# Norm factors from a halved root, and the first two row blocks scaled ahead of the middle's sum

## The chip, the core and the metric

One core of a Trainium2 chip runs the whole program. The metric is the device time of one execution in microseconds (us); smaller is better. Times come from unprofiled executions, the profile from one profiled execution of the same program.

## What is computed

A trunk of two layers over a sequence of 1024 rows of 1024 numbers. Layer 0 mixes by a gated linear recurrence (RG-LRU), layer 1 by stick-breaking attention; each is followed by a SwiGLU feed-forward part (FFN) of width 2816. Ahead of each of the four parts, and once more at the end, stands an RMS norm:

```python
def rms_norm(x, g):
    xf = x.astype(jnp.float32)
    y = xf * lax.rsqrt(jnp.mean(xf * xf, axis=-1, keepdims=True) + RMS_EPS)
    return (y * g.astype(jnp.float32)).astype(x.dtype)

def reference(...):
    h = x
    for layer in range(DEPTH):
        hn = rms_norm(h, mix_norm[layer])
        mixed = rg_lru_block(hn, ...) if layer % 2 == 0 else stick_breaking_attention(hn, ...)
        h = h + mixed
        h = h + swiglu_ffn(rms_norm(h, ffn_norm[layer]), ffn_w_in[layer], ffn_w_out[layer])
    return rms_norm(h, final_norm)
```

So for each of the 1024 rows, five times in the program, a sum of 1024 squares becomes one factor, the reciprocal root of (sum / 1024 + 1e-6). This text is about how the factors are worked out, and about the last of the five norms.

## The kernel before

**Layout.** The hidden state is kept turned: eight tiles of 128 columns (`h[d]`), each in two halves of 512 rows (`n`). Every product in fp32 is made as three matmuls of high and low parts (`mm3`, lines 141 to 143), so PE, the matmul engine, carries nearly all of the work. The queues of PE, ACT (ScalarE), DVE (VectorE) and POOL (GpSimd) run in the order in which the program is written; each engine takes its own instructions strictly in order. SP issues the DMAs.

**Sums.** Squares of `h` are added up over the column tiles in `acc` and `rbc`. What is left is a sum over 128 partitions; `stats` does it on PE, with the accumulated squares as weights and a column of ones (`st_ps`, line 203). The result stands in PSUM, one column for each block of 128 rows. `stats_mm` does the same in the FFN parts (line 956), and `row_factors` at the start takes sums that ACT has left in SBUF (`ssum`).

**Factors.** In all three a DVE instruction makes the mean square `ms` out of the sums (lines 207, 330, 964). `rstd` (line 174) then takes the root on ACT (178), its reciprocal on DVE (179), and three more DVE instructions make one step of Newton's iteration on the reciprocal (180 to 182). The last of them writes into `rcol`, one column for each row block. It runs nine times: twice at the start, once in each FFN part, twice at the start of the attention, three times at the end. In the first six cases PE later spreads the factors over all partitions (`rb_ps` line 188, `ob` line 969).

**The end.** `finish` does the last pair of column tiles and the last norm. `last` makes the final products of one column tile for a stretch of rows (`o_ps`) and then runs four instructions on them: the addition onto `h` on DVE (line 1283), the square on ACT (1284), the addition of the square into `acc` on DVE (1286), the multiplication by the norm's gain on ACT (1287). The stretches are `first` (rows 0 to 511), `mid` (the first two blocks of the second half) and `end` (its last two blocks), each for two column tiles. `turn` turns a block of 128 rows back by four transposes into one PSUM bank (`e_ps`, line 1293); `leave` scales it by its column of `rcol`, on DVE for even blocks (line 1304) and on ACT for odd ones (1302), and sends 256 KB to the output (1307). The order is written out by hand: the sums of `first` are taken inside the products of `mid`'s second tile (`ahead`), then come that tile's four instructions, then the left half of row blocks 0 to 3, then `end`'s first tile, the sums of `mid`, the right half of blocks 0 to 3, the left half of blocks 4 and 5, `end`'s second tile (its squares go into the last sums directly), one block that leaves, the last sums, and the rest. All `o_ps`, `st_ps` and `e_ps` tiles of this part come out of six PSUM banks.

Of the kernel before, what the change touches and what calls it, by code (L numbers as in the profile page):

```python
# [8 lines left out]
F32 = mybir.dt.float32  # L9
# [3 lines left out]
AF = mybir.ActivationFunctionType  # L13
ALU = mybir.AluOpType
PSUM = bass.MemoryType.PSUM

P = 128
S = 1024
D = 1024
ND = D // P  # L20
NT = S // P
# [6 lines left out]
EPS = 1e-6  # L28

V_MIX, V_FFN, V_FIN, V_BIN, V_CW, V_CB, V_GB, V_LAM, V_BO = 0, 16, 32, 40, 56, 88, 96, 112, 120  # L30
# [3 lines left out]
def trunk(  # L34
# [22 lines left out]
    nc = tc.nc  # L57
    f32 = lambda t: t.bitcast(F32)

    cp = ctx.enter_context(tc.tile_pool(name="cp", bufs=1))  # L60
# [31 lines left out]
    make_identity(nc, ident)  # L92
    ones = cp.tile([P, 1], F32, name="ones")
    nc.gpsimd.memset(ones, 1.0)
    vc = cp.tile([P, P], F32, name="vc")

    rbc = [cp.tile([P, NB], F32, name=f"rbc{n}") for n in range(NH)]
    acc = [None] * NH
# [8 lines left out]
    rcol = cp.tile([P, NT], F32, name="rcol")  # L107
# [32 lines left out]
    def mm3(ps, wh, wl, mh, ml, first, last, **kw):  # L140
        nc.tensor.matmul(ps, lhsT=wh, rhs=mh, start=first, stop=False, **kw)  # L141
        nc.tensor.matmul(ps, lhsT=wh, rhs=ml, start=False, stop=False, **kw)  # L142
        nc.tensor.matmul(ps, lhsT=wl, rhs=mh, start=False, stop=last, **kw)  # L143
# [27 lines left out]
            self.w[self.order[i]] = (k3(hi), k3(lo))  # L171


    def rstd(dst, ms):
        n = dst.shape[-1]
        sq = cp.tile([P, max(n, 4)], F32, tag="rs_s", name="rs_s", bufs=2)[:, 0:n]
        t = cp.tile([P, max(n, 4)], F32, tag="rs_t", name="rs_t", bufs=2)[:, 0:n]
        nc.scalar.sqrt(sq, ms)
        nc.vector.reciprocal(sq, sq)
        nc.vector.tensor_mul(t, sq, sq)  # L180
        nc.vector.scalar_tensor_tensor(t, t, -0.5, ms, op0=ALU.mult, op1=ALU.mult)
        nc.vector.scalar_tensor_tensor(dst, t, 1.5, sq, op0=ALU.add, op1=ALU.mult)

    def broadcast_r(ps_pool, tag, n):
        ps = ps_pool.tile([P, NB], F32, tag=tag, name="rb_ps")
# [12 lines left out]
    def stats(acc, ps_pool, tag, n, i0=0, i1=4):  # L198
        ps = ps_pool.tile([P, NB], F32, tag=tag, name="st_ps")
        accs = acc if isinstance(acc, tuple) else (acc,)  # L200
        for i in range(i0, i1):
            for a in accs:
                nc.tensor.matmul(
                    ps[:, i : i + 1], lhsT=a[:, i * P : (i + 1) * P], rhs=ones, start=a is accs[0], stop=a is accs[-1]
                )
        ms = cp.tile([P, 4], F32, tag="ms", name="ms", bufs=2)[:, i0:i1]
        nc.vector.tensor_scalar(ms, ps[:, i0:i1], 1.0 / D, EPS, op0=ALU.mult, op1=ALU.add)
        rstd(rcol[:, 4 * n + i0 : 4 * n + i1], ms)

    def squares(h, d, n, sqp, acc, eng=None, first=None):  # L210
        if d == 0 if first is None else first:
# [21 lines left out]
    def open_h(nm):  # L233
        hp = hstk.enter_context(tc.tile_pool(name=nm, bufs=1, side="right", reuse_waits="tile"))
        h = [[hp.tile([P, NB], F32, name=f"{nm}{d}_{n}") for n in range(NH)] for d in range(ND)]
        acc[:] = [hp.tile([P, NB], F32, name=f"acc{n}") for n in range(NH)]
        for j in range(ND // 2):
            for d in (j, j + ND // 2):
                for n in range(NH):
                    nc.sync.dma_start(h[d][n], hd[d][n])  # L240
        return h
# [13 lines left out]
    with ExitStack() as st, tc.manual_schedule(engines={E.PE, E.Activation, E.DVE, E.Pool, E.SP}):  # L255
        sp = st.enter_context(tc.tile_pool(name="sp", bufs=1))
# [41 lines left out]
                aw.append(load_raw(cols(w_in, c), (ND,)))  # L298

        ssum = sp.tile([P, NT], F32, name="ssum")  # L300
        ms = sp.tile([P, NT], F32, name="ms0")
        junk = sp.tile([P, D], F32, name="junk")
        pst = lambda name: sps.tile([P, NB], F32, tag="tp", name=name)
        k3 = lambda t: t.rearrange("p (k c) -> p k c", k=ND)
# [1 line left out]
        ps = pst("vps0")  # L306
# [20 lines left out]

        def row_factors(n):
            nn = slice(4 * n, 4 * n + 4)
            nc.vector.tensor_scalar(ms[:, nn], ssum[:, nn], 1.0 / D, EPS, op0=ALU.mult, op1=ALU.add)  # L330
            rstd(rcol[:, nn], ms[:, nn])


        def wsplit(i):
# [18 lines left out]
        for ks in (range(4), range(4, ND)):  # L353
            for lhs, rhs in ((0, xh), (0, xl), (1, xh)):
                for k in ks:
                    first, last = lhs == k == 0 and rhs is xh, lhs == 1 and k == ND - 1
# [22 lines left out]
        for r0, r1 in ((0, 32), (32, 64), (64, P)):  # L379
            ps = pst("vps")  # L380
# [11 lines left out]
    with ExitStack() as st:  # L392
        lp = st.enter_context(tc.tile_pool(name="lp", bufs=1, reuse_waits="tile"))
        psl.append(lst.enter_context(tc.tile_pool(name="psB", bufs=2, space=PSUM, reuse_waits="tile")))
        V = nc.vector
        lam = vc[:, V_LAM : V_LAM + ND]
        sm = lambda name: lp.tile([P, ND], F32, name=name)
        V = nc.vector
# [54 lines left out]
        ahead = {0: aw[2], D + 2 * P: aw[3]}  # L453


        turn = [0]
# [95 lines left out]
    h = open_h("h")  # L552
# [76 lines left out]
    def mix_out_ffn_in(h, mix, bias, layer, gnext, outs):  # L629
        w_in = ffn_w_in[layer]  # L630
        gcol = V_FFN + layer * ND
        V = nc.vector
# [12 lines left out]
        if outs:  # L645
# [15 lines left out]
            pp = Six()  # L661
        else:
            pp = ps_.enter_context(tc.tile_pool(name="fps", bufs=6, space=PSUM, reuse_waits="tile"))
# [107 lines left out]
        with tc.manual_schedule(engines={E.PE, E.Activation, E.DVE, E.Pool}):  # L771
# [12 lines left out]
            for j in range(HK):  # L784
                rows = (j, j + HK)
                dn = [(d, n) for d in rows for n in range(NH)] if j else [(d, n) for n in range(NH) for d in rows]
                for k, (d, n) in enumerate(dn):
                    o = HK * j + k
                    if (d, n) in begun:
                        ps = begun[d, n]  # L790
                        hi, lo = mix.w[d]
                        mm3(ps, hi[:, ND - 1], lo[:, ND - 1], xh[ND - 1][n], xl[ND - 1][n], False, True)
                    else:
                        ps = pp.tile([P, NB], F32, tag="p", name="ob_ps")
# [142 lines left out]
            ps = half(ob, 0)  # L937
# [14 lines left out]
            def stats_mm():  # L952
                st_ps = half(ob, 1)
                for n in range(NH):
                    for i in range(4):
                        nc.tensor.matmul(
                            st_ps[:, 4 * n + i : 4 * n + i + 1],
                            lhsT=acc[n][:, i * P : (i + 1) * P],
                            rhs=ones,
                            start=True,  # L960
                            stop=True,
                        )
                ms = cp.tile([P, NT], F32, tag="ms8", name="ms8", bufs=1)
                V.tensor_scalar(ms, st_ps[:, 0:NT], 1.0 / D, EPS, op0=ALU.mult, op1=ALU.add)
                rstd(rcol, ms)

            def factors():
                for b in range(NT):
# [151 lines left out]
            def weights_of(kind, x):  # L1120
                return weights_in(x, False) if kind == "f" else weights_out(x)

            last_use = {p: max(u for u, (_, p0, p1) in enumerate(VISITS) if p0 <= p < p1) for p in range(NF // 2)}
            for s_, (kind, x) in enumerate(steps):
                w, nw, ahead = nw, nxt, None
                if s_ + 2 < len(steps):
                    ahead = weights_of(*steps[s_ + 2])
                elif final and s_ + 2 == len(steps):
                    ahead = weights_out(NV - 1)
# [136 lines left out]
    def finish(h, w, R, pp, rows):  # L1266
        ys = {}
        d0, p0, p1 = 0, NF // 2 - 2, NF // 2


        def last(x, n, i0, i1, add=True, ahead=None):
            d, cs = d0 + x * HK, slice(i0 * P, i1 * P)
            ps = pp.tile([P, NB], F32, tag="p", name="o_ps")[:, cs]
            for k, p in enumerate(range(p0, p1)):
                for y in range(2):
                    if ahead and k + y == 2:
                        ahead()
                    hi, lo = w.a[("r", y) if x else y]
                    c = slice(k * P, (k + 1) * P)
                    rhs = [t[:, cs] for t in R[p][((0, 1), (7, 6))[n][y]]]  # L1280
                    mm3(ps, hi[:, c], lo[:, c], *rhs, k + y == 0, k + y == 2)
            t, sq, ac = h[d][n][:, cs], rbc[n][:, cs], acc[n][:, cs]
            nc.vector.tensor_add(t, ps, t)
            nc.scalar.square(sq, t)
            if add:
                nc.vector.tensor_add(ac, ac, sq)
            nc.scalar.activation(t, t, AF.Copy, scale=vc[:, V_FIN + d : V_FIN + d + 1])

        def turned(n, i, hf):
            ps = pp.tile([P, NB], F32, tag="p", name="e_ps")  # L1290
            for j in (1, 2, 3, 0):
                d = 4 * hf + j
                nc.tensor.transpose(ps[:, j * P : (j + 1) * P], h[d][n][:, i * P : (i + 1) * P], ident)
            return ps

        def leave(ps, n, i, hf):
            cs = slice(hf * NB, (hf + 1) * NB)
            b = 4 * n + i
            if hf == 0:
                ys[b] = rp.tile([P, D], F32, tag="raw", name="y") if b < 3 else rows[b - 3]  # L1300
            if i % 2:
                nc.scalar.activation(ys[b][:, cs], ps, AF.Copy, scale=rcol[:, b : b + 1])
            else:
                nc.vector.tensor_scalar_mul(ys[b][:, cs], ps, rcol[:, b : b + 1])

            queue = nc.scalar if (n, i, hf) == (1, 3, 1) else nc.sync
            queue.dma_start(out[0, b * P : (b + 1) * P, cs], ys[b][:, cs])

        def turn(n, i0, i1, hf):
            for i in range(i0, i1):  # L1310
                leave(turned(n, i, hf), n, i, hf)


        nc.scalar.sqrt(rcol[:, 0:1], ones)
        first, mid, end = (0, 0, 4), (1, 0, 2), (1, 2, 4)
        last(0, *first)
        last(1, *first)
        last(0, *mid)

        last(1, *mid, ahead=lambda: stats(acc[0], pp, "p", 0))  # L1320
        turn(*first, 0)
        last(0, *end)
        stats(acc[1], pp, "p", 1, 0, 2)
        turn(*first, 1)
        turn(*mid, 0)

        last(1, *end, add=False)
        held = [turned(1, i, 1) for i in range(2)]
        leave(held[0], 1, 0, 1)
        stats((acc[1], rbc[1]), pp, "p", 1, 2, 4)  # L1330
        leave(held[1], 1, 1, 1)
        turn(*end, 0)
        turn(*end, 1)
# [27 lines left out]
    with ExitStack() as st:  # L1361
# [257 lines left out]
        with tc.manual_schedule(engines={E.PE, E.Activation, E.DVE, E.Pool, E.SP}):  # L1619
# [3 lines left out]
            first = qkv_steps(0)  # L1623
# [50 lines left out]
    h = open_h("hh")  # L1674
# [44 lines left out]
```

## Time and profile before

| what | value |
|---|---|
| time, median of 3 runs | 2181.59 us (2181.5 to 2181.69) |
| time of the profiled execution | 2181.29 us |
| its span, first to last instruction | 2179.5 us |
| PE busy | 2165.6 us (99%) |
| DVE busy | 1703.6 us (78%) |
| ACT busy | 1077.0 us (49%) |
| POOL busy | 112.2 us (5%) |
| mean granted PE clock | 0.999 |

A row of the timeline reads: start in us from the span's start, duration in us, engine, line of the kernel, operation, output <- inputs, partitions x elements, number of instructions merged into the row; in brackets the idle time of the engine ahead of it and what ended it. PEld is the loading of matmul weights, which overlaps PE. A name with q (SPq) is the engine's instruction queue. A row of the windows reads: stretch, its length, busy time of each engine with its count of instructions, granted PE clock, share of time in which the DMA engines were busy, GB/s.

### The profile page before, as it was taken

The page shows a single profiled execution, that of the slowest core. Times are in us where ns is not written, and L with a number is a line of the kernel's source. Part 1 is how long each engine was busy: PE and PEld are TensorE (multiplying, and loading weights), DVE is VectorE, ACT ScalarE, POOL GpSimd, SP SyncE. Part 2 cuts the span into 40 slices and gives each one's busy share as a digit, 9 for nine tenths or more (in the row PEclk, how much of TensorE's full clock was granted, in tenths as well). Part 3 has the DMA queues.
Part 4 walks back from the last instruction along what each step waited for, and adds up shares of the span by engine and source line. Part 5 has one row for each costly group of instructions (what it writes and reads, how often), then busy time and mean ns, then how long its engine had stood idle before and what let it go on. Part 6 is the DMA issues. An engine that isn't in the chain of part 4 may idle for free.

```text
span 2179.5 us, 27426 instructions
## 1 busy us (share of the span) xinstructions
PE 2165.6 (99%) x10126; PEld 1802.2 (83%) x10126; DVE 1703.6 (78%) x2380; ACT 1077.0 (49%) x1765; POOL 112.2 (5%) x84
## 2 busy tenths in 40 slices
PE   8999999999999999999999999999999999999998
PEld 7888888888888888888888888888888888888887
DVE  7888777767777887887888888886877777788886
ACT  6677445334444544554555555553534444454556
POOL 1222020000000000000000000002000000000002
PEclk9999999999999999999999999999999999999999
DMA  7111412344444764434333344552133444467452
GB/s 233 49 49 39 135 39 73 103 125 157 138 146 139 248 222 130 146 121 101 98 97 93 95 105 107 147 193 57 53 116 122 146 145 145 141 232 233 138 153 89
DMA packets 296101, 277.64 MB, mean 127 GB/s; under 512 B 15256, under 2 KB 210976, under 8 KB 295968
## 3 DMA queue, kind: packets, MB, share of 16 engines
q1 hardware_dynamic: 295808, 275.64, 41.1%
q8 instruction: 79, 1.29, 0.3%
q14 instruction: 54, 0.44, 0.1%
q10 hardware_dynamic: 160, 0.27, 0.0%
HBM read 175.71 MB, written 74.97 MB: 115 GB/s over the span
## 4 chain that ended last, share of the span: by engine, by line
PE 96%; DVE 2%; ACT 1%; DMA 1%; issue 0%; SPq 0%; DVEq 0%; ACTq 0%
PE p_ps L143 18%; PE p_ps L141 18%; PE p_ps L142 18%; PE qk_ps L141 4%; PE qk_ps L143 4%; PE qk_ps L142 4%; PE wt_ps L1533 3%; PE a_ps L142 3%; PE a_ps L143 3%; PE a_ps L141 3%; PE ob_ps L141 3%; PE ob_ps L142 2%; PE ob_ps L143 2%; PE z_ps L1503 2%; PE z_ps L1504 2%; PE av_ps L1555 2%
## 5 line engine op out<-in xcount | busy, mean ns | idle before, releaser
L143 PE MATMUL p_ps<-vh,wbl 128*128 128x512 f32 x524 | 204.2, 390 | 0.2 <-DVE wbl L721 0.2
L143 PE MATMUL p_ps<-vh,wal 128*128 128x512 f32 x524 | 204.1, 389 | 0.1
L141 PE MATMUL p_ps<-vh,wbh 128*128 128x512 f32 x524 | 204.2, 390 | 0.0
L141 PE MATMUL p_ps<-vh,wch 128*128 128x512 f32 x524 | 204.1, 390 | 0.0
L143 PE MATMUL p_ps<-vh,wcl 128*128 128x512 f32 x524 | 204.1, 389 | 0.0
L142 PE MATMUL p_ps<-vl,wbh 128*128 128x512 f32 x524 | 203.9, 389 | 0.0
L142 PE MATMUL p_ps<-vl,wch 128*128 128x512 f32 x524 | 203.9, 389 | 0.0
L142 PE MATMUL p_ps<-vl,wah 128*128 128x512 f32 x524 | 203.9, 389 | 0.0
L141 PE MATMUL p_ps<-vh,wah 128*128 128x512 f32 x524 | 203.8, 389 | 0.0
L1542 ACT CAST th<-wt_ps 128x512 fp32r<-128x512 f32 x192 | 92.1, 480 | 209.6 <-PE wt_ps L1533 209.5
L717 ACT CAST wbh<-sb 128x1024 fp32r<-128x1024 f32 (+2 forms) x69 | 69.6, 1009 | 194.1 <-DVE sb L701 194.1
L1543 DVE TENSOR_TENSOR tl<-wt_ps,th 128x512 fp32r<-128x512 f32 x192 | 106.1, 552 | 62.9 <-ACT th L1542 61.1
L141 PE MATMUL qk_ps<-vh,whi 128*128 128x512 f32 x264 | 118.3, 448 | 0.0
L143 PEld LDWEIGHTS p_ps<-vh,wbl 128*128 128x128 f32 x524 | 98.4, 188 | 21.9 <-DVE wbl L721 1.5
L143 PEld LDWEIGHTS p_ps<-vh,wal 128*128 128x128 f32 x524 | 98.4, 188 | 21.4 <-DVE wal L712 1.0
L143 PEld LDWEIGHTS p_ps<-vh,wcl 128*128 128x128 f32 x524 | 98.4, 188 | 21.0 <-DVE wcl L731 0.6
L141 PEld LDWEIGHTS p_ps<-vh,wch 128*128 128x128 f32 x524 | 98.4, 188 | 20.5 <-ACT tb L1108 0.2
L141 PEld LDWEIGHTS p_ps<-vh,wbh 128*128 128x128 f32 x524 | 98.4, 188 | 20.4 <-ACT ta L1108 0.2
L142 PEld LDWEIGHTS p_ps<-vl,wah 128*128 128x128 f32 x524 | 98.4, 188 | 20.4
L141 PEld LDWEIGHTS p_ps<-vh,wah 128*128 128x128 f32 x524 | 98.4, 188 | 20.4
L142 PEld LDWEIGHTS p_ps<-vl,wbh 128*128 128x128 f32 x524 | 98.4, 188 | 20.3
L142 PEld LDWEIGHTS p_ps<-vl,wch 128*128 128x128 f32 x524 | 98.4, 188 | 20.3
(353 smaller groups left out, 5568.2 us busy)
## 6 DMA issues: line engine op xcount, KB each, us to landing
raw<-in_ffn_w_in SPq DMA_DIRECT2D x88, 512.0 KB, 4.0
vl<-pd SPq DMA_DIRECT2D x128, 256.0 KB, 3.5
pd<-U SPq DMA_DIRECT2D x90, 256.0 KB, 2.3
kk<-two SPq DMA_DIRECT2D x64, 256.0 KB, 3.9
raw<-in_ffn_w_out SPq DMA_DIRECT2D x56, 256.0 KB, 3.4
raw<-in_attn_w_qkv SPq DMA_DIRECT2D x24, 512.0 KB, 4.3
q<-two SPq DMA_DIRECT2D x64, 128.0 KB, 2.3
raw<-in_lru_w_in SPq DMA_DIRECT2D x15, 512.0 KB, 4.1
```

The costliest lines, as they stand in the source:

```text
L141: nc.tensor.matmul(ps, lhsT=wh, rhs=mh, start=first, stop=False, **kw)
L142: nc.tensor.matmul(ps, lhsT=wh, rhs=ml, start=False, stop=False, **kw)
L143: nc.tensor.matmul(ps, lhsT=wl, rhs=mh, start=False, stop=last, **kw)
L717: nc.scalar.copy(self.full(self.wb), self.full(self.sb))
L1503: nc.tensor.matmul(ps[:, 0 : c1 - c0], lhsT=lhsT, rhs=KK[q][hx][:, 0, c0:c1], start=True, stop=False)
L1504: nc.tensor.matmul(ps[:, 0 : c1 - c0], lhsT=lhsT, rhs=KK[q][hx][:, 1, c0:c1], start=False, stop=True)
L1533: nc.tensor.transpose(tp[:, c : c + P], W[q, hx, j, kb // 4][:, (kb % 4) * P : (kb % 4 + 1) * P], ident)
L1542: nc.scalar.copy(th[:, q0:], tp[:, q0:])
L1543: nc.vector.tensor_sub(tl[:, q0:], tp[:, q0:], f32(th)[:, q0:])
L1555: nc.tensor.matmul(ps[:, q0:], lhsT=VV[q][:, kb, hx], rhs=tl[:, q0:], start=False, stop=last)
```

## The change

It has two parts.

**The factors.** The DVE instruction that made the mean square is gone from all three callers, and `rstd` gets the sums themselves. ACT takes the root of a quarter of the mean square straight from the sums: it scales by 0.25/1024 and adds a quarter of epsilon from a new constant column `eps4`, which POOL fills at the start. DVE makes the same quarter in a tile of its own, takes the reciprocal of the root, multiplies the quarter by it, adds the root, and takes the reciprocal of that. With m the mean square and r about sqrt(m)/2, (m/4)/r + r is Newton's step for sqrt(m).

**The end.** `last` no longer runs its four instructions itself but returns them as a function, which most callers call at once. For `mid`'s second tile they are put between the row blocks: blocks 0 and 1 leave first, then the four instructions run, then blocks 2 and 3 leave.

```diff
+    eps4 = cp.tile([P, 1], F32, name="eps4")
+    nc.gpsimd.memset(eps4, 0.25 * EPS)
...
-    def rstd(dst, ms):
+    def rstd(dst, sums):
         n = dst.shape[-1]
-        sq = cp.tile([P, max(n, 4)], F32, tag="rs_s", name="rs_s", bufs=2)[:, 0:n]
-        t = cp.tile([P, max(n, 4)], F32, tag="rs_t", name="rs_t", bufs=2)[:, 0:n]
-        nc.scalar.sqrt(sq, ms)
-        nc.vector.reciprocal(sq, sq)
-        nc.vector.tensor_mul(t, sq, sq)
-        nc.vector.scalar_tensor_tensor(t, t, -0.5, ms, op0=ALU.mult, op1=ALU.mult)
-        nc.vector.scalar_tensor_tensor(dst, t, 1.5, sq, op0=ALU.add, op1=ALU.mult)
+        quarter, root = (cp.tile([P, max(n, 4)], F32, tag=x, name=x, bufs=2)[:, 0:n] for x in ("rs_m", "rs_s"))
+        nc.scalar.activation(root, sums, AF.Sqrt, scale=0.25 / D, bias=eps4)
+        nc.vector.tensor_scalar(quarter, sums, 0.25 / D, 0.25 * EPS, op0=ALU.mult, op1=ALU.add)
+        nc.vector.reciprocal(dst, root)
+        nc.vector.tensor_mul(quarter, quarter, dst)
+        nc.vector.tensor_add(quarter, quarter, root)
+        nc.vector.reciprocal(dst, quarter)
...
-        ms = cp.tile([P, 4], F32, tag="ms", name="ms", bufs=2)[:, i0:i1]
-        nc.vector.tensor_scalar(ms, ps[:, i0:i1], 1.0 / D, EPS, op0=ALU.mult, op1=ALU.add)
-        rstd(rcol[:, 4 * n + i0 : 4 * n + i1], ms)
+        rstd(rcol[:, 4 * n + i0 : 4 * n + i1], ps[:, i0:i1])
...
-            nc.vector.tensor_scalar(ms[:, nn], ssum[:, nn], 1.0 / D, EPS, op0=ALU.mult, op1=ALU.add)
-            rstd(rcol[:, nn], ms[:, nn])
+            rstd(rcol[:, nn], ssum[:, nn])
...
-                ms = cp.tile([P, NT], F32, tag="ms8", name="ms8", bufs=1)
-                V.tensor_scalar(ms, st_ps[:, 0:NT], 1.0 / D, EPS, op0=ALU.mult, op1=ALU.add)
-                rstd(rcol, ms)
+                rstd(rcol, st_ps[:, 0:NT])
...
-            t, sq, ac = h[d][n][:, cs], rbc[n][:, cs], acc[n][:, cs]
-            nc.vector.tensor_add(t, ps, t)
-            nc.scalar.square(sq, t)
-            if add:
-                nc.vector.tensor_add(ac, ac, sq)
-            nc.scalar.activation(t, t, AF.Copy, scale=vc[:, V_FIN + d : V_FIN + d + 1])
+
+            def rest():
+                t, sq, ac = h[d][n][:, cs], rbc[n][:, cs], acc[n][:, cs]
+                nc.vector.tensor_add(t, ps, t)
+                nc.scalar.square(sq, t)
+                if add:
+                    nc.vector.tensor_add(ac, ac, sq)
+                nc.scalar.activation(t, t, AF.Copy, scale=vc[:, V_FIN + d : V_FIN + d + 1])
+
+            return rest
...
-        last(0, *first)
-        last(1, *first)
-        last(0, *mid)
-
-        last(1, *mid, ahead=lambda: stats(acc[0], pp, "p", 0))
-        turn(*first, 0)
-        last(0, *end)
+        last(0, *first)()
+        last(1, *first)()
+        last(0, *mid)()
+
+        rest = last(1, *mid, ahead=lambda: stats(acc[0], pp, "p", 0))
+
+        turn(0, 0, 2, 0)
+        rest()
+        turn(0, 2, 4, 0)
+        last(0, *end)()
         stats(acc[1], pp, "p", 1, 0, 2)
...
-        last(1, *end, add=False)
+        last(1, *end, add=False)()
```

More of the change, by code (lines that the diff above doesn't have):

```diff
@@ L300, in trunk @@
         ssum = sp.tile([P, NT], F32, name="ssum")
-        ms = sp.tile([P, NT], F32, name="ms0")
         junk = sp.tile([P, D], F32, name="junk")
```

## The prediction

> **What bounds the kernel now.** I read the page first, then the list of waits with PE as the waiting engine.
>
> ```profile
> span 2179.5 us, 27426 instructions
> ## 1 busy us (share of the span) xinstructions
> PE 2165.6 (99%) x10126; PEld 1802.2 (83%) x10126; DVE 1703.6 (78%) x2380; ACT 1077.0 (49%) x1765; POOL 112.2 (5%) x84
> ```
>
> ```profile
> PE vps L307 <- DMA vmix<-in_mix_norm: 3.2, 1, 3.2
> PE tp L313 <- DMA xt<-in_x: 2.5, 2, 1.3
> PE wt_ps L1533 <- DVE tl L1543: 1.2, 3, 0.7
> PE z_ps L1503 <- DMA kk<-two: 1.0, 1, 1.0
> PE p_ps L143 <- DVE wbl L721: 0.2, 1, 0.2
> ```
>
> That is the whole list: PE is idle for 13.9 us, 8.1 us of it in these five waits, and none of them is for `rcol`, for `rb_ps` or for `ob`. So in the first six of its nine runs `rstd` is hidden: no PE instruction waits for a factor. A gain can only come from the three runs at the end, where the last one stands alone. Next I read the timeline of the end, DVE alone, then ACT.
>
> ```profile
> 2172.24 0.16 DVE L207 TENSOR_SCALAR ms<-st_ps 128x2 f32<-128x2 f32 x1 [0.61 <-PE st_ps L203]
> 2172.67 0.17 DVE L179 RECIPROCAL rs_s<-rs_s 128x2 f32<-128x2 f32 x1 [0.27 <-ACT rs_s L178]
> 2172.87 0.16 DVE L180 TENSOR_TENSOR rs_t<-rs_s 128x2 f32<-128x2 f32 x1
> 2173.06 0.16 DVE L181 SCALAR_TENSOR_TENSOR rs_t<-rs_t,ms 128x2 f32<-128x2 f32 x1
> 2173.26 0.16 DVE L182 SCALAR_TENSOR_TENSOR rcol<-rs_t,rs_s 128x2 f32<-128x2 f32 x1
> 2173.53 1.41 DVE L1304 TENSOR_SCALAR U<-e_ps,rcol 128x512 f32<-128x512 f32 x2
> ```
>
> ```profile
> 2172.43 0.20 ACT L178 ACTIVATE rs_s<-ms 128x2 f32<-128x2 f32 x1 [0.57 <-DVE ms L207]
> 2172.54 0.67 ACT L1302 ACTIVATE U<-e_ps,rcol 128x512 f32<-128x512 f32 x1
> ```
>
> From the mean square to the first scaled block are 1.29 us (2172.24 to 2173.53): six short instructions in a row, each some 0.04 us behind the one that it needs. A dependent DVE step costs 0.20 us from start to start. Is the end set by this chain or by the 4 MB of output? The windows answer, with the DMA share next to last in each row:
>
> ```profile
> 2174.00:2175.00 1.00, 0.00 (x1) 0.00 (x0) 0.94 (x2) 0.78 (x2) 0.00 (x0) 1.00 0.84 313
> 2175.00:2176.00 1.00, 0.00 (x0) 0.00 (x0) 0.00 (x0) 0.00 (x0) 0.00 (x0) 1.00 0.87 322
> ```
>
> The DMA engines are idle for about 0.29 us (0.16 + 0.13) just after the last blocks are scaled. Their backlog is gone before the last four transfers come, so these start when they are issued. The chain sets the end, and a microsecond of it is a microsecond of the time.
>
> **The change part by part: the factors.** Removed are one DVE step ahead of the root (0.16 us and a hand-over of 0.04) and two later ones; added are the quarter, an addition and a second reciprocal. DVE has five steps as before. What counts is where the quarter stands. It reads the same PSUM tile as the root, and the trace has such a pair at the start, where ACT and DVE both read `tp`:
>
> ```profile
> 6.48 0.69 DVE L320 COPY hc<-tp 128x512 f32<-128x512 f32 x1 [2.83 <-ACT xh L316]
> ```
>
> The copy takes nothing from `xh`, yet it is held until ACT is done with `tp`. I take it that the quarter is held by the root in the same way. [...] If the two ran side by side, each chain would be 0.08 us shorter than below.
>
> The root itself gets a bias operand in SBUF. The nearest rows for an operand of that kind are the square and the gain multiplication of 256 columns:
>
> ```profile
> 2161.95 0.51 ACT L1287 ACTIVATE hh<-hh,vc 128x256 f32<-128x256 f32 x1
> 2162.54 0.21 ACT L178 ACTIVATE rs_s<-ms 128x4 f32<-128x4 f32 x1
> 2163.92 0.42 ACT L1284 ACTIVATE rbc<-hh 128x256 f32<-128x256 f32 x1 [1.17 <-DVE hh L1283]
> ```
>
> 0.51 - 0.42 = 0.09 us for the pointer, so the root takes between 0.20 and 0.29 us; I take 0.29, because the operand is of that kind. The reciprocal of the root needs nothing from the quarter, so it follows at the spacing of independent steps:
>
> ```profile
> 2163.39 0.16 DVE L182 SCALAR_TENSOR_TENSOR rcol<-rs_t,rs_s 128x4 f32<-128x4 f32 x1
> 2163.47 0.42 DVE L1283 TENSOR_TENSOR hh<-o_ps,hh 128x256 f32<-128x256 f32 x1
> 2164.37 0.43 DVE L1286 TENSOR_TENSOR acc<-acc,rbc 128x256 f32<-128x256 f32 x1 [0.48 <-ACT rbc L1284]
> 2164.71 1.40 DVE L1304 TENSOR_SCALAR y<-e_ps,rcol 128x512 f32<-128x512 f32 x2
> ```
>
> The addition onto `hh` starts 0.08 us after the factor. So the last chain becomes root 0.29, hand-over 0.04, quarter 0.08, three dependent steps 0.60, and 0.27 + 0.02 to the scaling (2173.26 to 2173.53, and a reciprocal is 0.01 to 0.02 longer): 1.30 us against 1.29. Sum for this part: +0.01 us; with a root of 0.20 us, -0.08.
>
> [...]
>
> Elsewhere the same step costs nothing as long as the six hidden chains stay hidden. The constant column is one more small POOL instruction ahead of PE's first wait of 3.2 us. No DMA is added.
>
> **The change part by part: the end.** Moved are two scalings (DVE for block 0, ACT for block 1) with their two output DMAs on SP, ahead of four instructions. The order on SP stays the same; its first two outputs leave earlier.
>
> The root of `first`'s sums can start a little before ACT's gain multiplication ends (2161.95 + 0.51 = 2162.46; overlap 0.09 by the pair 2172.43 and 2172.54), at 2162.37. Then 0.29 + 0.04 + 0.08 + 0.60 brings the last reciprocal to 2163.38, where the factor stood before (2163.39). Block 0's scaling can start at 2163.65 (+ 0.27). That is 1.06 us earlier than now; but the additions for `mid`, which fill that time now, come later for it. Two scalings take 1.40 us, the second starts 0.66 after the first, so the addition comes to 2164.31 instead of 2163.47. From there to the addition into `acc` (2164.37) it is 0.90 and on to the next scaling 0.34: block 2 at 2165.55, where it now stands at 2164.71 + 0.66 = 2165.37. DVE is 0.18 us late: the scaling starts 0.27 after the factor's instruction, where the addition started 0.08 after it.
>
> Does DVE have that much slack? Its later rows and PE's:
>
> ```profile
> 2166.03 0.41 DVE L1283 TENSOR_TENSOR hh<-o_ps,hh 128x256 f32<-128x256 f32 x1
> ...
> 2168.36 1.40 DVE L1304 TENSOR_SCALAR y<-e_ps,rcol 128x512 f32<-128x512 f32 x2
> 2169.68 0.74 DVE L1304 TENSOR_SCALAR G<-e_ps,rcol 128x512 f32<-128x512 f32 x1
> 2170.44 0.42 DVE L1283 TENSOR_TENSOR hh<-o_ps,hh 128x256 f32<-128x256 f32 x1
> ```
>
> ```profile
> 2164.28 0.36 PE L141 MATMUL o_ps<-vh,wah 128*128 128x256 f32 x1
> ...
> 2168.73 0.36 PE L141 MATMUL o_ps<-vh,wrh 128*128 128x256 f32 x1
> ...
> 2171.37 0.30 PEld L203 LDWEIGHTS st_ps<-ones,rbc 128*128 128x128 f32 x2
> ```
>
> The addition at 2166.03 follows block 2's scaling back to back (2165.37 + 0.66), so it comes to 2166.21. From it to the scaling at 2168.36 are 2.33 us, and the second factor chain lies in between. There the root starts 0.11 earlier against the gain (it no longer waits for `ms`), takes 0.09 longer and the quarter's slot is 0.08 more: 2.40 us with rounding up, so 2168.61, or 0.25 late. Three scalings at 0.66 then bring the addition of the last products to 2170.59, against 2170.44. It stood 0.10 behind DVE's earliest time (2168.36 + 1.98 = 2170.34), which is the slack. On this addition hang the square and then the last sums on PE (2171.37, 0.93 later). Sum for this part: +0.15 us; between 0 (root of 0.20) and +0.34 (no overlap of ACT's instructions, 0.09 and 0.10 more).
>
> **Sum:** +0.01 + 0.15 = +0.16 us on the profiled execution: span 2179.7, time 2181.29 + 0.16 = 2181.45. The median of the runs is 0.30 above that execution (2181.59), so 2181.75, rounded to 2181.8.
>
> **The rivals.**
>
> *The reads run side by side, or DVE's slack suffices.* Then both early chains are 0.08 shorter, the lateness of 0.25 falls to 0.09, below the slack of 0.10, and the last chain is 1.22: 0.07 us faster, 2181.5. Against it stands the held copy of `tp`.
>
> *The output sets the end.* Two transfers start 1.06 us earlier; if the writes were the limit, most of that would come back: 0.8 us, the time of one transfer of 256 KB at the 313 to 322 GB/s above, 2180.8. Against it stand the idle 0.29 us.
>
> *PE waits for a bank (slower).* `end`'s first products start at 2164.28. If they got the bank of `mid`'s second tile, they would have to wait for the moved addition, until 2164.31 + 0.42 + 0.04 = 2164.77, and PE would be 0.49 us late to the end: 2182.1. It decides from the point where that addition ends later than 2164.24. With six banks in strict rotation it would be that bank. But the trace does not rotate strictly: the products at 2168.73 would then have taken the bank of a block whose scaling runs until 2168.36 + 0.74 = 2169.10. Banks go to whoever finds one free, and the one of the sums is.
>
> *DVE stands still at the start of the attention (slower).*
>
> ```profile
> 967.10 1.49 DVE L1257 TENSOR_TENSOR rbc<-rbc,acc 128x512 f32<-128x512 f32 x2
> ```
>
> ```profile
> 968.67 0.20 ACT L178 ACTIVATE rs_s<-ms 128x4 f32<-128x4 f32 x1
> ```
>
> ```profile
> 969.67 0.95 PE L203 MATMUL st_ps<-ones,rbc 128*128 128x1 f32 x8
> ```
>
> These two additions stand behind the mean square now, and ACT's root comes only at 968.67. If the quarter takes the place of the mean square on DVE, it holds the additions until 968.67 + 0.29 + 0.04 + 0.08 = 969.08, they end at 970.57, and PE's second sums wait 0.94 us: with the rest 2182.7. If they stay ahead of it, or if the root moves forward with the sums, it costs nothing to 0.3 us.
>
> [...]
>
> **How the numbers follow.** 0.2% of this time, about what a measurement of this kernel can tell from no change, is 4.4 us; no case above comes near it. Chances: forecast with its bounds 0.55, side by side or slack enough 0.15, bank 0.1, attention 0.1, empty pipe 0.05, output 0.05. The likeliest time is 2181.8. The range runs from 2181.2 (the second case less a few tenths for single executions) to 2182.4 (bank and pipe cases, and the attention's smaller price); it leaves out the output case and the attention at its full price. Faster by over 0.2%: 0.01, slower: 0.02 (a stall that no row shows), within: 0.97.
>
> **What would show it.** In the profile after, the root on ACT straight behind `st_ps` with 0.25 to 0.3 us; the quarter behind it with ACT as releaser, not beside it; 0.08 us from quarter to reciprocal. Block 0 scaled at about 2163.6, `mid`'s addition behind it near 2164.3, `end`'s first products still at 2164.3, the last addition of products near 2170.6 instead of 2170.4. The DMA share at 2166 to 2167 higher and the gap ahead of the last four transfers wider, without gain. I am wrong if PE shows a new wait, if the quarter runs during the root, or if the output ends earlier than its last scaling explains.

## The result: 34.6 us slower, in a place the prediction does not name

| | before | after |
|---|---|---|
| time, median of 6 runs | 2181.55 us | 2216.14 us (2215.28 to 2216.35) |
| span of the profiled execution | 2179.5 us | 2214.5 us |

The ratio is 1.0159, 95% interval 1.0149 to 1.0168. The prediction had 2181.2 to 2182.4 us. The page of the profile after:

```profile
span 2214.5 us, 27430 instructions
PE 2200.5 (99%) x10126; PEld 1801.8 (81%) x10126; DVE 1701.4 (77%) x2380; ACT 1078.1 (49%) x1765; POOL 114.0 (5%) x85
```

and its list of waits with PE as the waiting engine (us in total, times, longest):

```profile
PE tp L314 <- DMA xt<-in_x: 3.6, 2, 1.9
PE vps L308 <- DMA vmix<-in_mix_norm: 2.4, 1, 2.4
PE wt_ps L1538 <- DVE tl L1548: 1.2, 3, 0.7
PE z_ps L1508 <- DMA kk<-two: 0.9, 1, 0.9
PE p_ps L145 <- DVE wbl L721: 0.2, 1, 0.2
```

The waits are the same five, 8.3 us against 8.1. PE does the same 10126 matmuls at the same granted clock (0.999), and is busy for 34.9 us more. So nothing new waits; the matmuls themselves have become slower. The windows show where: one row of before, then the same stretch of after (PE's busy time, with the count in brackets, is the first column behind the length).

```profile
360.00:660.00 300.00, 300.00 (x1333) 248.71 (x1332) 218.14 (x282) 123.70 (x184) 0.00 (x0) 1.00 0.42 134
```

```profile
360.00:660.00 300.00, 300.00 (x1319) 244.44 (x1318) 211.79 (x280) 123.80 (x184) 0.00 (x0) 1.00 0.39 127
```

In these 300 us of the FFN nothing of the change runs in before, and in after only the six short steps of one factor, at 366 us, for which PE does not wait; yet PE gets 14 matmuls less done. The groups of instructions (busy us, mean ns of one) show which kinds; before, then after:

```profile
L142 PE MATMUL p_ps<-vl,wch 128*128 128x512 f32 x524 | 203.9, 389 | 0.0
L141 PE MATMUL a_ps<-xh,whi 128*128 128x512 f32 x248 | 97.1, 391 | 0.0
L1533 PE MATMUL wt_ps<-ident,w 128*128 128x128 f32 x576 | 94.2, 272 | 1.2 <-DVE tl L1543 1.2
```

```profile
L144 PE MATMUL p_ps<-vl,wch 128*128 128x512 f32 x524 | 206.3, 394 | 0.0
L143 PE MATMUL a_ps<-xh,whi 128*128 128x512 f32 x248 | 98.6, 398 | 0.0
L1538 PE MATMUL wt_ps<-ident,w 128*128 128x128 f32 x576 | 94.2, 272 | 1.2 <-DVE tl L1548 1.2
```

Matmuls overlap: in before the next one starts 227 ns behind a product with 512 columns (median of the trace), so a mean of 391 ns is not what one costs; its rise by 5 to 7 ns is close to how much later the next one starts (5.3 ns, experiment 6). Products with streams of 512 columns pay it (389 to 394 and 391 to 398 ns); the transposes (`wt_ps`) do not (272 ns in both).

The change touches those products in one way only. It drops the tiles `rs_t`, `ms` and `ms8` from the constants pool `cp` and adds `eps4` and `rs_m`, and by the addresses that the tiles get, each of their buffers takes 32 bytes of every partition: 160 bytes less (five buffers), 96 more (three). Pools on the left side of SBUF are stacked on `cp`, so all of them (raw weights, `xh` and `xl`, half of the `v` tiles, `xg`) move down by 64 bytes. The split weights and the other half of the `v` tiles are stacked from the right end and stay. Two tiles that nothing reads set the places of both stacks: `edge_l` at the end of `cp` and `edge` at the right end. Matmul by matmul, TensorE streams 512 columns of `v`, `x` or `xg` (2048 bytes in a partition) against weights of 128 columns.

### The profile page after: what moved, and what is told of

Read it like the earlier page. It is cut to its first block, busy times and chain, and to the rows that moved or that the text cites. A ratio compares the mean times of both kernels' runs of the same rounds, so it can differ in the third digit from the quotient of the medians.

```text
span 2214.5 us, 27430 instructions
## 1 busy us (share of the span) xinstructions
PE 2200.5 (99%) x10126; PEld 1801.8 (81%) x10126; DVE 1701.4 (77%) x2380; ACT 1078.1 (49%) x1765; POOL 114.0 (5%) x85
## 3 DMA queue, kind: packets, MB, share of 16 engines
q8 instruction: 79, 1.29, 0.2%
## 4 chain that ended last, share of the span: by engine, by line
PE 98%; DVE 1%; DMA 1%; ACT 0%; issue 0%; SPq 0%; DVEq 0%; ACTq 0%
PE p_ps L144 19%; PE p_ps L143 19%; PE p_ps L145 19%; PE qk_ps L143 4%; PE qk_ps L145 4%; PE qk_ps L144 4%; PE wt_ps L1538 3%; PE a_ps L144 3%; PE a_ps L145 3%; PE a_ps L143 3%; PE ob_ps L143 3%; PE ob_ps L145 3%; PE ob_ps L144 3%; PE z_ps L1508 2%; PE av_ps L1560 2%; PE z_ps L1509 2%
```

## The experiments

**1. The shift alone, and the change without it.** Theory A: the 64 bytes cost everything. Rival B: the new instructions do.

```diff
--- before, e1_shift
-    cp.tile([P, 120], F32, name="edge_l")
+    cp.tile([P, 104], F32, name="edge_l")
```

> The kernel before with one edit: the unused padding tile edge_l in the constants pool is [P,104] instead of [P,120], so every pool on the left side of SBUF lies 64 bytes lower, exactly where the change puts it. No instruction is changed. Theory A (the change costs its 34.6 us because its smaller constants pool moves the operands of the matmuls by 64 bytes): 2216 us, PE busy 2200 us instead of 2165.6, no new wait on PE. Rival B (the new instructions of the factors or of the end cost it): 2181.6 us, PE busy 2165.6.

```diff
--- after, e2_restored
-    cp.tile([P, 120], F32, name="edge_l")
+    cp.tile([P, 136], F32, name="edge_l")
```

> The kernel after with one edit: edge_l is [P,136] instead of [P,120], so that every pool on the left side lies where it did before the change. All new instructions stay. Theory A: 2181.4 to 2181.9 us, PE busy 2165.6 again; what is left against before is the pure price of the edit, forecast at +0.16 us, or -0.07 if the last chain is as short as the trace after shows it (root to scaling 1.22 us). Rival B: 2216 us.

The shift alone: 2216.18 us, ratio 1.0161 (1.0147 to 1.0175). The whole change with its tiles back in place: 2181.32 us, 1.0001 (0.9992 to 1.0010). PE's line of the shift alone, then of the restored change:

```profile
PE 2200.6 (99%) x10126; PEld 1801.9 (81%) x10126; DVE 1702.0 (77%) x2380; ACT 1077.9 (49%) x1765; POOL 115.3 (5%) x84
```

```profile
PE 2165.6 (99%) x10126; PEld 1802.1 (83%) x10126; DVE 1702.8 (78%) x2380; ACT 1077.0 (49%) x1765; POOL 112.6 (5%) x85
```

One unused tile, made 64 bytes smaller, gives the whole loss without any line of the change, and 64 bytes of padding take it all away. Rival B is gone.

**2. Each half alone, in place.** The end without the new factors (the last two hunks of the diff, on before), and the factors without the new end (the rest of it, with `edge_l` at [P,136]).

> The kernel before with only the end of the change: blocks 0 and 1 are scaled and sent ahead of the additions of the middle's sum; the factors are computed as before, and the constants pool has its old size. Theory A: 2181.6 to 2181.9 us (the prediction's end part is +0.15 us, of it 0.04 to 0.1 without the new factor chain). Rival B in the form that the reordered end costs it: 2216 us. In the profile block 0 is scaled about 1 us earlier and the last scaling comes 0 to 0.2 us later.

> The kernel before with only the new factors (root from the sums, Newton's step on the root), edge_l at [P,136] so that every pool lies where it did before. Theory A: 2181.4 to 2181.7 us (the prediction has +0.01; the trace after suggests -0.07). Rival B in the form that the factor chain costs it: 2216 us.

End alone 2181.46 us, 0.9999 (0.9990 to 1.0008); factors alone 2180.91 us, 0.9999 (0.9990 to 1.0008). Neither half differs from before by what these runs can tell, about 2 us; single executions of each lie between 2179 and 2183 us. Which of the terms of a tenth of a microsecond is right can be read from the traces only (below).

**3. Which rule of place?** With 64 bytes less, the streams start at another place modulo 128, and so does their distance to the weights. Four more shifts of before:

```diff
--- before: e5_both64 | e6_right64 | e7_left32 | e8_left128
-    edge.tile([P, 24], F32, name="edge")        # right end
+    edge.tile([P, 8], ...)     | [P, 8]  | [P, 24] | [P, 24]
-    cp.tile([P, 120], F32, name="edge_l")       # left
+    cp.tile([P, 104], ...)     | [P, 120]| [P, 112]| [P, 88]
```

> The kernel before with edge_l at [P,104] and the right side's padding tile edge at [P,8]: the pools on both sides of SBUF are moved by 64 bytes, so the 512-column streams of TensorE (left: x, lower v, xg; right: upper v) and the weights (right) have again the same place to each other modulo 128. Theory A1 (a stream costs more if it starts at 64 modulo 128, whatever the weights do): the lower pools cost 35 us as in the first experiment (about 5300 matmuls, 6.6 ns each) and the upper v another 3474 x 6.6 ns = 23 us, 2240 us. Theory A2 (it costs more if streams and weights disagree modulo 128): 2181.5 us.

> The kernel before with only the right side moved by 64 bytes (edge at [P,8]): weights and upper v start at 64 modulo 128, x, lower v and xg at 0. A1 (the stream's own start): only the upper v pays, 3474 x 6.6 ns = 23 us, 2204 us; matmuls on x (a_ps<-xh) stay at 391 ns. A2 (disagreement): x, lower v and xg pay 35 us, 2216 us, a_ps<-xh at 398 ns, the upper v nothing. A3 (the weights' start): all of them pay, 58 us, 2240 us.

> The kernel before with edge_l at [P,112]: the left pools lie 32 bytes lower, their streams start at 96 modulo 128. If any start off the multiple of 128 bytes costs one piece more, the time is that of the 64-byte shift, 2216 us. If the cost grows with the distance it is between 2190 and 2216. If only multiples of 32 are needed: 2181.5 us.

> The kernel before with edge_l at [P,88]: the left pools lie 128 bytes lower. If the rule is the start modulo 128, it costs nothing: 2181.5 us. If it is any place other than the tuned one (the distance between pools, or modulo 256 or more), it costs up to the 35 us of the 64-byte shift: 2190 to 2216 us.

| kernel | left moved | right moved | distance changed by | time, us | ratio, 95% |
|---|---|---|---|---|---|
| e1 | -64 | 0 | -64 | 2216.18 | 1.0147 to 1.0175 |
| e6 | 0 | +64 | -64 | 2214.75 | 1.0126 to 1.0185 |
| e5 | -64 | +64 | -128 | 2210.90 | 1.0108 to 1.0167 |
| e8 | -128 | 0 | -128 | 2209.60 | 1.0102 to 1.0161 |
| e7 | -32 | 0 | -32 | 2211.44 | 1.0111 to 1.0170 |

No rule that I had written down fits. In e8 every start is again what it was modulo 128, and it loses over 28 us: the second outcome of its expectation. e5 gives neither 2240 nor 2181.5; stream and weights agree there modulo 128 again, but a smaller tile at the right end moves the right side up, so they are 128 bytes further apart. In the group of the product on `x`, of e6 and then of e8:

```profile
L141 PE MATMUL a_ps<-xh,whi 128*128 128x512 f32 x248 | 98.6, 398 | 0.0
```

```profile
L141 PE MATMUL a_ps<-xh,whi 128*128 128x512 f32 x248 | 98.3, 396 | 0.0
```

e6 leaves `x` where it was and moves only the weights, yet it gives the 398 ns of the shift alone. Sorted by the change of distance, pairs fall together. So a fourth theory, A4: what counts is the distance from stream to weights, with a period of more than 128 bytes. In before it is 0 modulo 256 for each of the 8790 products with 512 columns, by the addresses that the kernel's tiles get.

**4. The test of the distance.** Both sides moved by 64 bytes the same way (all starts change, no distance does), and the left side alone moved by 256.

```diff
--- before: e9_both_same | e10_left256
-    edge.tile([P, 24], F32, name="edge")        # right end
+    edge.tile([P, 40], ...)       | [P, 24]
-    cp.tile([P, 120], F32, name="edge_l")       # left
+    cp.tile([P, 104], ...)        | [P, 56]
```

> The kernel before with both sides moved by 64 bytes in the same direction: edge_l at [P,104] moves the left pools down by 64, the right side's edge at [P,40] moves the right pools down by 64. All starts change, the distances between left and right pools do not. Theory A4 (the cost goes with the distance in bytes between stream and weights, which the earlier shifts all changed: by 64, 128, 64, 32 and 128 bytes): 2181.5 us, a_ps<-xh back at 391 ns. If starts themselves count, modulo 128 or 256 or otherwise: 2205 us or more, a_ps<-xh at 396 to 398 ns.

> The kernel before with edge_l at [P,56]: the left pools lie 256 bytes lower, the right ones stay. If the distance counts modulo 256: 2181.5 us. If it counts modulo 512 or more, or if only the tuned place is good: 2205 to 2216 us.

e9: 2182.02 us, 1.0001 (0.9992 to 1.0011). e10: 2181.06 us, 0.9997 (0.9987 to 1.0008). The same group, of e9 and of e10:

```profile
L141 PE MATMUL a_ps<-xh,whi 128*128 128x512 f32 x248 | 97.0, 391 | 0.0
```

```profile
L141 PE MATMUL a_ps<-xh,whi 128*128 128x512 f32 x248 | 97.0, 391 | 0.0
```

Both are as before. In e9 the left tiles lie exactly where the shift alone has them. So in these runs the time goes with the distance and not with the starts: 2182.02 and 2181.06 us where it changed by 0 and by 256 bytes, 2209.60 to 2216.18 us where it changed by 32, 64 or 128.

**5. The cost by itself.** One matmul form, nothing else, the distance set by the first column of the slices:

```python
for k in range(96):
    a, b = w // 4 + P * (k % 8), m // 4 + NB * (k % 4)   # w, m: bytes; P = 128, NB = 512
    nc.tensor.matmul(ps, lhsT=W[:, a : a + P], rhs=M[:, b : b + NB], start=True, stop=True)
```

> A kernel that leaves the whole computation out and only measures the disputed cost: groups of 96 matmuls of 512 columns in the same form as the kernel's, eight weight tiles in turn, four streams in turn, nothing else running. Bytes by which stream and weights are moved from a place where they agree modulo 512: da 0/0, db 0/32, dc 0/64, dd 0/96, de 0/128, df 0/192, dg 0/256, dh 0/384, di 64/64, dj 64/0, dk 128/128, dl 32/32, dm 0/16, dn 0/0 (stream/weights). Theory A4 with modulo 256: 227 ns a matmul in da, dg, di, dk, dl, dn; 233 ns in the others. With modulo 512: dg as the others too. Starts alone (A1): da to dh, dm 227 ns, di, dj, dl 233. In the last six groups VectorE copies beside it from a tile at the same place (va), at 64, 128 and 256 (vb, vc, vd), with the stream at 64 (ve) and with its output at 64 (vf): if other engines' accesses collide in the same way, vb, vc and vf are slower than va; the slices without other engines in the big kernel say they are not.

The groups of instructions of the one execution (busy us of 96, mean ns):

```profile
L83 PE MATMUL db<-mv,wt 128*128 128x512 f32 x96 | 22.7, 395 | 0.0
L83 PE MATMUL dd<-mv,wt 128*128 128x512 f32 x96 | 22.7, 396 | 0.0
L83 PE MATMUL dc<-mv,wt 128*128 128x512 f32 x96 | 22.6, 395 | 0.0
L83 PE MATMUL dm<-mv,wt 128*128 128x512 f32 x96 | 22.6, 395 | 0.0
L83 PE MATMUL dh<-mv,wt 128*128 128x512 f32 x96 | 22.5, 395 | 0.0
L83 PE MATMUL de<-mv,wt 128*128 128x512 f32 x96 | 22.5, 395 | 0.0
...
L83 PE MATMUL df<-mv,wt 128*128 128x512 f32 x96 | 22.1, 391 | 0.0
L83 PE MATMUL dj<-mv,wt 128*128 128x512 f32 x96 | 22.1, 391 | 0.0
...
L83 PE MATMUL dk<-mv,wt 128*128 128x512 f32 x96 | 22.0, 389 | 0.0
...
L83 PE MATMUL dl<-mv,wt 128*128 128x512 f32 x96 | 22.0, 389 | 0.0
L83 PE MATMUL dn<-mv,wt 128*128 128x512 f32 x96 | 21.9, 389 | 0.0
L83 PE MATMUL di<-mv,wt 128*128 128x512 f32 x96 | 21.9, 389 | 0.0
L83 PE MATMUL dg<-mv,wt 128*128 128x512 f32 x96 | 21.9, 389 | 0.0
```

Read as stream less weights: at 0 (dn, di, dk, dl, and dg at -256) 389 ns (da, at 0 too, is left out: a matmul of db came in ahead of it); at -16, -32, -64, -96, -128 and -384 (dm, db, dc, dd, de, dh) 395 or 396, which is 0.6 to 0.8 us more for 96, 6 to 8 ns each. In df (-192) and dj (+64) the distance is +64 modulo 256, and there it is 0.2 us, 2 ns each. By the starts in the trace, one comes 227 ns after the other at 0, 232 to 234 at the first kind of distance, 229 at +64. That the sign matters was in no expectation. The copies on VectorE ran earlier than meant, beside the warm-up group wu, da and db, so the last six groups say nothing about other engines.

**6. The rest of the loss.** The shifted kernel has its 10126 matmuls in the order of before, so the time from each start to the next can be compared one by one. Of 35.0 us, 26.5 are lost in 4956 streams of 512 columns at -64 (5.3 ns each), 8.0 in 3834 whose own distance has not changed (2.1 ns each), and 0.5 in shorter streams. (The 3834 are 3450 streams of the upper `v` and 384 in the attention, where stream and weights both lie on the left; the counts of 5300 and 3474 in the expectations above were too high.) A last kernel, again only matmuls with the weights at one place, asks why the second kind loses. Its distance of -64 is made as +192, which is the same modulo 256:

```python
i = k // run % len(ms)     # which of the two places ms[0], ms[1] this matmul streams from
a, b = P * (k % 8), ms[i] // 4 + NB * (k % 4)
nc.tensor.matmul(ps[i], lhsT=W[:, a : a + P], rhs=M[:, b : b + NB], start=True, stop=True)
```

> A second kernel that leaves the computation out and measures the cost by itself: groups of 96 matmuls of 512 columns, weights at 0 modulo 256. It asks why, in the shifted kernels, some streams whose own distance to the weights is unchanged (the upper v, about 7 of the 35 us) are slower too. Theory N (neighbours: a stream at a bad distance slows the ones after it): in ja/kb, jc/kd and je/kf streams at 0 (j) and at -64 (k) take turns after 1, 3 and 12 matmuls; the j then are slower than the 389 ns of ha, most in ja. Theory E (other engines: VectorE's or ScalarE's tiles at a bad distance from PE's stream): hb, he, hg, with VectorE, ScalarE or both emptying the previous group's PSUM tile into a tile at 0, stay at 389 ns, while hc, hf, hh (the same at 64) and hd, hi (at 128) take 391 ns or more. If neither shows, the 7 us stay open. hj (stream at -64, alone) should take 395 ns, hk (with both engines at 64 too) as much or more.

Its groups, from one execution:

```profile
L93 PE MATMUL hj<-mv,wt 128*128 128x512 f32 x96 | 22.6, 394 | 0.0
...
L93 PE MATMUL ha<-mv,wt 128*128 128x512 f32 x96 | 21.9, 389 | 0.0
...
L93 PE MATMUL hf<-mv,wt 128*128 128x512 f32 x96 | 21.9, 389 | 0.0
L93 PE MATMUL hg<-mv,wt 128*128 128x512 f32 x96 | 21.9, 389 | 0.0
L93 PE MATMUL hh<-mv,wt 128*128 128x512 f32 x96 | 21.9, 389 | 0.0
...
L93 PE MATMUL jg<-mv,wt 128*128 128x512 f32 x48 | 11.8, 391 | 0.0
L93 PE MATMUL je<-mv,wt 128*128 128x512 f32 x48 | 11.6, 390 | 0.0
```

Theory E shows nothing: with VectorE and ScalarE at work every group at 0 stays at 389 (the two engines took turns on the one PSUM tile and ran behind their groups, so which offset ran beside which group is blurred; none of them shows a cost). hj, at +192, has a start every 233 ns, as dc at -64 had. Theory N holds, as an after-effect. Only je/kf and jg/kh took turns as written; the other two pairs came out mostly in one block each. In je, the first matmuls after a turn at -64 start 226, 236, 228, 233, 231 ns apart, and from then on 226 or 227: some 20 ns for each return to a good distance. In the shifted kernel's trace (e1) the same series stands behind the returns from -64 to 0, about 480 of them; 480 x 20 ns = 9.6 us is about the 8.0 us found, as over a quarter of the stretches at 0 are shorter than five matmuls. The after-effect was not of one size in the runs compared: taken in the same way, e7 (-32) loses 26.1 us in the moved streams but only 4.0 in the others, e8 (-128) 20.6 and 8.3, which is why the totals of the table differ. In e11 it shows without a group at a bad distance too: dl follows dk, both at 0 but with starts that differ modulo 256, and its first nine starts are 224 to 236 ns apart.

## Why the prediction was wrong

**The step that failed** is the first one, and it was never written as a step: PE's busy time of 2165.6 us was carried into the sum unchanged. The change was costed by its instructions (five DVE steps for five, one more POOL instruction for `eps4`), not by the bytes of the tiles that it drops and adds. All the rivals are waits or ends of chains; none is a slower matmul. "A stall that no row shows" had a chance of 0.02, and it was no stall: PE's waits are what they were. The row that could have priced it was not in before, since there every product has distance 0; but that the left pools would move, and that nothing in the trace bounds what that costs, could have been said. e1 measured 35.0 us for the shift (2216.18 against 2181.19 for before).

**The rest of the sum** can be judged in e2, where the layout is as before. ACT first, then DVE:

```profile
2162.94 0.51 ACT L1287 ACTIVATE hh<-hh,vc 128x256 f32<-128x256 f32 x1
2163.35 0.25 ACT L181 ACTIVATE rs_s<-st_ps,eps 128x4 f32<-128x4 f32 x1
...
2173.26 0.26 ACT L181 ACTIVATE rs_s<-st_ps,eps 128x2 f32<-128x2 f32 x1 [0.38 <-PE st_ps L207]
```

```profile
2163.64 0.16 DVE L182 TENSOR_SCALAR rs_m<-st_ps 128x4 f32<-128x4 f32 x1 [0.28 <-ACT rs_s L181]
2163.72 0.17 DVE L183 RECIPROCAL rcol<-rs_s 128x4 f32<-128x4 f32 x1
...
2164.32 0.18 DVE L186 RECIPROCAL rcol<-rs_m 128x4 f32<-128x4 f32 x1
2164.60 0.75 DVE L1306 TENSOR_SCALAR y<-e_ps,rcol 128x512 f32<-128x512 f32 x1
2165.27 0.41 DVE L1283 TENSOR_TENSOR hh<-o_ps,hh 128x256 f32<-128x256 f32 x1
...
2171.47 0.42 DVE L1283 TENSOR_TENSOR hh<-o_ps,hh 128x256 f32<-128x256 f32 x1
...
2174.48 1.41 DVE L1306 TENSOR_SCALAR U<-e_ps,rcol 128x512 f32<-128x512 f32 x2
```

The gain multiplication that stood at 2161.95 is at 2162.94 here, because the start's waits for DMA were longer in this execution (`tp` and `vps`: 6.5 us against 5.7); so 0.99 is taken off.

| step | forecast | e2 less 0.99 |
|---|---|---|
| root starts | 2162.37 | 2162.36 |
| root's duration (three chains) | 0.29 | 0.25, 0.24, 0.26 |
| block 0 scaled | 2163.65 | 2163.61 |
| `mid`'s addition | 2164.31 | 2164.28 |
| last addition of products | 2170.59 | 2170.48 (before 2170.44) |
| last chain, from its first instruction to the scaling | 1.30 | 1.22 (before 1.29) |
| last scaling | 2173.69 (2173.53 + 0.16) | 2173.49 (before 2173.53) |

The quarter is held by the root, with ACT as its releaser and 0.28 us idle; the reads did not run side by side. The reciprocal follows 0.08 us behind it. No run shows the 0.20 us for this step that the empty-pipe case in the range and the chances stands for: the quarter and the reciprocal start 0.08 us apart in each of the three chains of e2. The root was oversized by 0.03 to 0.05 us in each of the three chains, and the rounding up of the steps behind it did the rest: the end comes 0.04 us earlier, not 0.16 later, in the single executions compared. The output case is out too: the windows of e2 (DMA share next to last) leave the DMA engines idle for 0.33 + 0.08 = 0.41 us behind the last scalings, where it was 0.29.

```profile
2175.00:2176.00 1.00, 0.03 (x1) 0.00 (x0) 0.89 (x2) 0.75 (x2) 0.00 (x0) 1.00 0.67 256
2176.00:2177.00 1.00, 0.00 (x0) 0.00 (x0) 0.00 (x0) 0.00 (x0) 0.00 (x0) 1.00 0.92 340
```

At the attention the quarter is held until 969.05 in e2 and lets only one of the two additions wait behind it (the second row); PE has no new wait there.

```profile
969.05 0.16 DVE L182 TENSOR_SCALAR rs_m<-st_ps 128x4 f32<-128x4 f32 x1 [0.68 <-ACT rs_s L181]
...
969.61 0.69 DVE L1255 TENSOR_TENSOR rbc<-rbc,acc 128x512 f32<-128x512 f32 x1
```

`end`'s products found a free bank: the list of PE's waits in e2 has the same five rows, and none is for `o_ps`.

## What to carry to other kernels

A change of a few small tiles moves every pool that is stacked on theirs (here by 64 bytes, for 35 us), so the bytes belong in the list of what a change removes and adds, next to its instructions; padding put the old distances back here without touching an instruction (e2, 2181.32 us). When PE is busy longer with the same count, the same clock and the same waits, compare the mean durations of its groups, and then where their operands lie. Try the layout by itself, with one unused tile, before reading a change's other effects.

## What the runs showed of the hardware

- In these runs a matmul that streams 512 columns of 4 bytes took about 227 ns from start to start with its stream and its weights a multiple of 256 bytes apart (e11: di, dk, dl, dn, dg), 232 to 234 ns with the stream 16, 32, 64, 96, 128 or 384 bytes below the weights or 192 above (e11, hj of e12), and 229 ns with it 64 above or 192 below (dj, df). With both starts moved alike nothing changed: 227 ns in di, dk and dl, 2182.02 us for the kernel in e9; nor with 256 bytes more between them, 2181.06 us in e10.
- Behind streams at -64, made as +192, the first five good ones lost some 20 ns together (je of e12).
- Over this kernel that was 28 to 35 us of 2181, for changes of the distance by 32, 64 or 128 bytes (e1, e5 to e8).
- Open, and shown by no run: whether the weights in use or those loaded for the next matmul count, why the sign matters, and why 256 bytes more cost nothing where 128 do. Inside each group the weights kept one place modulo 256, so only the ends of the groups of e11 bear on the first question. The last matmuls of da, dg and dk, at 0 themselves but with the next weights at another distance from their stream, are followed after 235, 233 and 236 ns, which speaks for the next weights; of the two opposite ends, dm to dn (225 ns) agrees and df to dg (236 ns) does not. These are single starts.
